# One decoder layer on one core: the gate r's last weight sum moved to a plain load and VectorE, its second step's blocks together, and the convolution's side work paced anew

## The chip, the cores and the metric

The kernel runs on 1 core of one Trainium2 chip. The metric is the device time of one execution in microseconds (us); lower is better. The kernel before took 844.33 us, the median of 3 runs (843.4 to 845.39). Engines are named as the profile names them: PE is TensorE, DVE is VectorE, ACT is ScalarE, POOL is GpSimd, SP is SyncE, which here only starts DMA transfers.

## The reference

One layer (DEPTH is 1) on 512 tokens of width 1024, all float32:

```
u = rmsnorm(x, norm1_g)
a_glu, q, k, v, r, g_low, gate_a, gate_b = split(u @ w_in)
c = a_glu[:, :1024] * sigmoid(a_glu[:, 1024:])
c = silu(layernorm(causal_dwconv(c, width 31)))          # convolution branch
o = gated linear attention, 4 heads, chunks of 64 (q, k, v, decay of g_low)
o = rmsnorm_per_head(o) * gla_norm_g * silu(r)            # r is the output gate
h = x + (sigmoid(gate_a) * (c @ w_conv_out) + sigmoid(gate_b) * (o @ w_gla_out)) @ w_o
h = h + ffn(rmsnorm(h, norm2_g));   out = rmsnorm(h, final_g)
```

The change lies in r = u @ w_r (1024 by 1024), in the depthwise convolution's taps beside the heads, and in the LayerNorm over channels that follows the convolution.

## The kernel before, in words

**Products in three terms.** Every float32 product is made of three fast ones: an operand x is split in a high half (ACT casts it to `whi`, L374 or L404) and a low half (DVE subtracts, `wlo`, L375 or L409); `mm3` (L463 to L469) issues low times high, high times low and high times high. So each weight block costs one ACT cast and one DVE subtraction before PE can use it. A flat list `order` (L213 to L243) says in which order weight blocks are loaded; `load` (L250) issues a block's DMA on SP's queue into one of 4 `raw` buffers, `refill` (L268) keeps up to 4 blocks (2 where marked tight) loaded ahead of the split ones, `split_weight` (L362) splits the next one into one of 4 `whi` and 4 `wlo` buffers, and `weight` (L427) hands a block to a product and splits up to LOOK = 2 ahead.

**Seven products in place of eight.** For r, w_o and w_down, `seven` (L1319) computes a 2 by 2 block product with seven block products (Winograd's form). Tokens are halved, the contraction is halved, the output columns are halved. The steps are a11, a12, s1, n2, s4, n3 and a22; each needs a sum of activation blocks (`token_sums_7`, L1137, on DVE and ACT) and a sum of weight blocks. Every step has two parts, d = 0 and 1, each with its own weight block (128 by 1024) that covers two pairs of contraction rows. A step with both parts at once makes 24 products of 512 columns; the list `STEPS` (L57) takes a11 whole, then a12 d0, s1 d0, a12 d1, s1 d1, and then n2, s4, n3, a22, each whole.

**The weight sums of r.** With W11, W12, W21, W22 the four blocks: a11 loads W11 into a `kept` buffer. After its split, POOL starts accumulating DMAs that add W12 to it (`sum_on`, L332, and `add_dram`, L297; for w_r each sum goes in two transfers of 256 KB). s1 uses that sum. a12 uses W21, loaded into `raw`. For n2, DVE adds the loaded W22 to `kept` (L329), giving W11 + W12 + W22; after n2's split POOL again starts accumulating DMAs, W21 on top, and a22 uses the result. s4 uses W22 alone, still in its `raw` buffer. n3 loads W12 into `raw`, and POOL's DMAs add W22. So POOL issues twelve transfers for r: four for s1, four for n3, four for a22.

**After each step** `put_r` (L1410) moves or combines the PSUM banks: ACT copies a11, s1, n2 (L1413); for a12, s4 and n3 DVE combines (L1420), ACT takes silu (L1421), DVE multiplies into the attention output `ot` (L1422); for a22 ACT takes silu from PSUM (L1416) and DVE multiplies. n2, n3 and a22 share one pair of banks, so a22's first product waits until n3's combination has read them. `weight` calls of a22 are placed after n3's second combination (`freed`, L1359). While r runs, sums of activations wait in `urgent`, and `fill` (L447) takes them ahead of convolution work.

**The convolution** is depthwise, width 31, on DVE: 44 taps per channel tile at half the tokens (L807; 0.6 share each; ACT starts each of the three sums, L803), three closing adds (L821 to L825), eight tiles. The taps are queued in `chains`, and every `weight` call hands out some with `fill`: `share` units, 5.0 (RATE) by default, 2.5 for the paired tiles, 2.0 for w_r. When the eighth tile is done, `add_chain` sums the eight tiles (L858, L861) on DVE, and `norm_chain` (L929) follows: `ln_parts` splits the sum (L920, L921), `ln_mean` multiplies it by -1/1024 on PE (L889), `ln_center` subtracts and squares per tile (L892 to L898), `ln_var` and `ln_rstd` make and spread the root (L868, L876), `ln_out` scales, takes silu and splits (L910 to L921). norm_chain is held (`hold`, L444) until `start_norms` (L1470), which runs in the third quarter of the first `pair_7`. Empty entries `(2.5, lambda: None)` in a chain are pauses.

**Order around the change.** Four heads (L1263 to L1281): queries and keys of head h, scores and outputs of head h - 1 on PE, the last three GLU tiles between. Then four `gate_b` tiles, r by `seven`, and from `pair_7(0)` on the gates of the merge in paired tiles: each pair loads two blocks ("x1": one, two), POOL adds up the other three (L346, `two_sums`), and PE takes them as x1, x3, x2, x4. In pair 0, `gated_o` transposes the attention output (L1115) and splits it to `oa` (L1122, L1123); then come w_gla tiles 0 and 1, and pair 1. `oa` number 3 lives in the buffer in which the taps' second operand `aside` stands, so it waits for the last tap. A scheduler decides the final order on each engine, except where `issue_after` and `keep_in_program_order` bind it; semaphores follow from it.

Of the kernel before, what the change touches and what calls it, by code (L numbers as in the profile page):

```python
# [37 lines left out]
R_PAIRS = ((0, 4), (1, 5), (2, 6), (3, 7))  # L38
# [9 lines left out]
RATE = 5.0  # L48
# [7 lines left out]

STEPS = [("a11", 0), ("a11", 1), ("a12", 0), ("s1", 0), ("a12", 1), ("s1", 1)]  # L57
STEPS += [(step, d) for step in ("n2", "s4", "n3", "a22") for d in (0, 1)]
START = {ET.PE, ET.Activation, ET.DVE, ET.SP}


# [16 lines left out]
def trunk_layer(ctx: ExitStack, tc: tile.TileContext, a: dict, out: bass.AP):  # L78
# [30 lines left out]
    def tmp(n=T):  # L109
        return tp.tile([P, n], F32, tag="tmp", name=nm("tmp"), bufs=6)  # L110
# [102 lines left out]
    order = [("w_v", j) for j in range(KT // 2)]  # L213
# [6 lines left out]
        if h:  # L220
            order += glu_order[KT - LATE_GLU + h - 1]
    order += [("w_gb", m) for m in range(AHEAD)]
    order += [("w_r", (R_PAIRS, step, d)) for step, d in STEPS]
    tight = set()
    first = len(order)
    for (name, p, q), behind in zip(MERGE, BEHIND):
# [48 lines left out]
    def raw_tile():  # L275
        return wp.tile([P, D], F32, tag="raw", name=nm("raw"), bufs=4)


    def block(name, pairs, d, row, col):

        pairs = pairs[2 * d : 2 * d + 2]
        first = pairs[0][row]
        if name == "w_r":
            tiles = a[name][4 * col : 4 * col + 4, :, first * P : (first + 2) * P]
            return tiles.rearrange("m p c -> p m c")
        w = a[name][col * SEVEN[name] + first // 2]
        return w if len(pairs) == 2 else w[:, row * T : (row + 1) * T]

    def keep_tile(name):
        if name in ("w_o", "w_r"):  # L290
            return tp.tile([P, D], F32, tag="x", name=nm("kept"), bufs=3)
        return fp.tile([P, D], F32, tag="kept", name=nm("kept"), bufs=2)
# [9 lines left out]
    LOADS = {"a11": (0, 0), "a12": (1, 0), "n2": (1, 1), "n3": (0, 1)}  # L302

    def load_block(name, pairs, step, d):

        if step not in LOADS:
            return None
        src = block(name, pairs, d, *LOADS[step])
        n = D if name == "w_r" else src.shape[-1]
        if step == "a11":  # L310
            dst = keep_tile(name)[:, :n]
            kept[pairs, d] = dst
        else:
            dst = raw_tile()[:, :n]
        load_dma = nc.sync.dma_start(shaped(name, dst), src)
        if name == "w_down":
            tc.keep_in_program_order(load_dma)
        if step == "n3":
            add_dram(name, dst, block(name, pairs, d, 1, 1))
        if step == "n2":  # L320
            kept[pairs, d, "b22"] = dst
        return dst

    def operand(raw, pairs, step, d):

        if step == "s4":
            return kept[pairs, d, "b22"]
        if step == "n2":
            nc.vector.tensor_tensor(kept[pairs, d], kept[pairs, d], raw, ALU.add)  # L329
        return raw if step in ("a12", "n3") else kept[pairs, d]  # L330

    def sum_on(name, pairs, step, d):  # L332

        if step in ("a11", "n2"):
            nxt = block(name, pairs, d, *((0, 1) if step == "a11" else (1, 0)))
            add_dram(name, kept[pairs, d], nxt)

# [89 lines left out]
    def weight(name, j, ahead=LOOK):  # L427
        assert order[used[0]] == (name, j)
        prefetch(1)
        used[0] += 1  # L430
        prefetch(ahead)
        share = {"two": 2.5, "w_glu": RATE + 0.75, "w_r": 2.0}.get(name, RATE)

        fill(share + (1.75 if order[min(len(ready), len(order)) - 1] in ADDED else 0))
        return ready[used[0] - 1]
# [4 lines left out]
    after, urgent, hold, conv_given = [], [], [True], []  # L440
# [6 lines left out]
    def fill(n):  # L447
        room[0] += n
        while (urgent or chains) and room[0] > 0:
            chain = urgent or chains[0]  # L450
            share, work = chain.pop(0)
            room[0] -= share
            with ExitStack() as order_of:
                for ins in (pace[0], *behind):
                    order_of.enter_context(tc.issue_after(ins.ins))
                work()
            if chains and not chains[0]:
                chains.pop(0)
                start_chain()
        if not chains and not urgent:  # L460
            room[0] = 0.0
# [108 lines left out]

    start = tc.manual_schedule(engines=START)
    start.__enter__()
# [355 lines left out]

    def norm_chain():  # L929
        chain = [(RATE, ln_parts)]  # L930
        chain.append((0, ln_mean))
        chain.extend((2, lambda k=k: ln_center(k)) for k in range(KT))
        chain += [(2.5, lambda: None)] * 4
        chain.append((RATE, ln_var))
        chain.append((2.5, lambda: None))
        chain.append((0, ln_rstd))
        chain.extend((2.5, lambda k=k: ln_out(k)) for k in range(KT))
        return chain
# [8 lines left out]
    raw = tmp()  # L947
# [313 lines left out]
    s1_n2, of_s1, s4, of_n2, of_s4, n3, of_n3 = merge_sums  # L1261
# [57 lines left out]
    def seven(name, pairs, acts, complete, at=lambda step, i: None, fine=False, put=None, before=lambda step: None):  # L1319
# [30 lines left out]
                    read = 2 * d + j == len(acts) - 1  # L1350
                    mm3(acc, (ah, al), w_, opens and d == 0 and j == 0, read, not opens)

        steps = list(STEPS)
        while steps:
            step, d = steps.pop(0)
            if d == 0:
# [7 lines left out]
            half, n, op, whole = into[step]  # L1364
# [71 lines left out]
    def pair_7(n):  # L1436
        (name, p, q), behind = MERGE[n], BEHIND[n]
        unit = two_tiles(name, p, q, lambda: merge_acts, mm_bank, len(behind) < 3)
        if behind and behind[0][0] == "w_conv":
            while chains:  # L1440
                fill(1)
        for j in range(4):
            while urgent and j and len(urgent) > (5 if j == 1 else 0):
                urgent.pop(0)[1]()
            done = next(unit)
            if n == 0 and j in (1, 2):
                for m in range(2 * j - 2, 2 * j):
                    gated_o(m, ax_bank)
                if j == 2:
                    start_norms()  # L1450
            if j == 0 or n >= 3:

                while complete_pairs:
                    complete_pairs.pop(0)()
            if j == 3:
                third_ahead()

                def sigmoids(done=done):
                    for m, c in zip((p, q), done):
                        (part if name == "w_gb" else gas)[m] = sigmoid(m, c)  # L1460

                complete_pairs.append(sigmoids)
                if n >= 3:
                    complete_pairs.pop()()
            for proj, m, half in behind[j : j + 1]:
                open_tiles[proj, m] = tile_of(proj, m, half_of[half], open_tiles.get((proj, m)))
# [37 lines left out]
    for p, q in O_PAIRS:  # L1504
# [6 lines left out]
        s1, n2, n3, s4 = e1[:, :H], e1[:, H:], e2[:, :H], e2[:, H:]  # L1511
# [201 lines left out]
    for gi, pairs in enumerate(GROUPS):  # L1713
        acts = []
        if gi == 0:
# [3 lines left out]
            for j, lo in [(j, lo) for lo in (0, H) for j in range(3)]:  # L1719
                late = {(1, 0): (KT - 1, 2), (2, 0): (MID, 3)}.get((j, lo))  # L1720
                at = {late[0]: lambda t=late[1]: to_channels(normed[t], u2, t)} if late else {}
# [6 lines left out]
            s1_n2, of_s1, s4, of_n2, of_s4, n3, of_n3 = sums  # L1728
# [135 lines left out]
```

## Time and profile before

| | |
|---|---|
| median of 3 runs | 844.33 us (843.4 to 845.39) |
| the profiled execution | 841.78 us, span 840.0 us |
| mean granted TensorE clock | 0.988 |
| PE busy | 809.8 us, 96% of the span |
| DVE busy | 713.6 us, 85% |
| ACT busy | 467.9 us, 56% |
| POOL busy | 171.1 us, 20% |
| HBM traffic | 137 GB/s over the span |

The profiled execution has 1.78 us around its span. The span's stages, by the windows of the trace: loading and v to about 43 us, GLU tiles with the taps, v and decay to about 113, the four heads to about 208, gate_b to 236, r from 236 to 292, pair 0 and the first two w_gla tiles to about 318, then the other gates, w_conv, w_o and the channel mixer. A row of the timeline gives start, duration, engine, line, operation, output and inputs, and in brackets how long the engine sat idle before it and what released it. A duration there includes the tail that overlaps the next instruction; start to start is a little shorter.

### The profile page before, as it was taken

The numbers are of one execution on the slowest core, as the hardware profiler recorded it, in microseconds if no ns is written. First come the engines' busy times: TensorE is split into PE (matmuls) and PEld (weight loads), VectorE is DVE, ScalarE is ACT, GpSimd is POOL, SyncE is SP. The second block draws the span as 40 slices with busy tenths as digits, with TensorE's granted clock in tenths as the row PEclk, the third lists the DMA queues.
The fourth block names the chain that finished last, engine by engine and source line by source line (L and its number), as shares of the span: only waits on it lengthen the run. The fifth ranks groups of instructions, "written<-read, shape, count | busy, mean of one in ns | idle before, by whom it ended". The sixth has DMA issues, their size and how long they took to land.

```text
span 840.0 us, 11519 instructions
## 1 busy us (share of the span) xinstructions
PE 809.8 (96%) x4263; PEld 698.1 (83%) x4263; DVE 713.6 (85%) x1162; ACT 467.9 (56%) x690; POOL 171.1 (20%) x157
## 2 busy tenths in 40 slices
PE   9999999999998498999999999999999999999996
PEld 7888887888886387999988898899889988899885
DVE  6789999999877597576768889988974999779895
ACT  6654684764554454495444556546534664456654
POOL 2011011212122323323200110221212311422012
PEclk9999999999999699999999999999999999999999
DMA  8488868648455222325248732135663266424662
GB/s 331 136 199 190 217 155 195 145 108 200 76 101 125 42 96 89 101 76 176 92 139 214 207 101 80 47 101 181 130 165 101 89 168 144 139 98 153 177 126 100
DMA packets 38680, 115.70 MB, mean 138 GB/s; under 512 B 3848, under 2 KB 11152, under 8 KB 38624
## 3 DMA queue, kind: packets, MB, share of 16 engines
q1 hardware_dynamic: 27856, 85.34, 29.5%
q0 software_dynamic: 10752, 29.63, 21.0%
q8 instruction: 33, 0.54, 0.3%
q14 instruction: 23, 0.19, 0.1%
q10 hardware_dynamic: 16, 0.00, 0.0%
HBM read 112.86 MB, written 2.10 MB: 137 GB/s over the span
## 4 chain that ended last, share of the span: by engine, by line
PE 74%; DVE 17%; issue 3%; ACT 2%; POOL 2%; DMA 1%; POOLq 0%; SPq 0%; DVEq 0%; ACTq 0%
PE mm L467 21%; PE mm L468 21%; PE mm L469 21%; DVE c L807 6%; DVE aside L807 3%; PE mm L681 3%; PE ax L469 2%; PE ax L467 2%; PE ax L468 2%; DVE wlo L375 2%; POOL raw L346 1%; DMA raw<-in_w_v_dram 1%; DMA kept<-in_w_r_dram 1%; DVE h L842 0%; PE ax L1077 0%
## 5 line engine op out<-in xcount | busy, mean ns | idle before, releaser
L467 PE MATMUL mm<-uh,wlo 128*128 128x512 f32 (+1 forms) x608 | 220.1, 362 | 0.0
L468 PE MATMUL mm<-ul,whi 128*128 128x512 f32 (+1 forms) x608 | 218.1, 359 | 0.0
L469 PE MATMUL mm<-uh,whi 128*128 128x512 f32 (+1 forms) x608 | 217.8, 358 | 0.0
L469 PEld LDWEIGHTS mm<-uh,whi 128*128 128x128 f32 x608 | 115.4, 190 | 17.0
L467 PEld LDWEIGHTS mm<-uh,wlo 128*128 128x128 f32 x608 | 115.6, 190 | 16.6
L468 PEld LDWEIGHTS mm<-ul,whi 128*128 128x128 f32 x608 | 115.5, 190 | 16.3
L375 DVE TENSOR_TENSOR wlo<-raw,whi 128x1024 fp32r<-128x1024 f32 x86 | 100.2, 1171 | 33.6 <-ACT whi L374 29.8
L346 POOL TENSOR_TENSOR raw<-raw,raw 128x512 f32<-128x512 f32 x42 | 66.9, 1592 | 235.4 <-DVE wlo L375 152.7
L374 ACT CAST whi<-raw 128x1024 fp32r<-128x1024 f32 x86 | 82.4, 964 | 37.0 <-PE mm L469 26.6
L404 ACT CAST whi<-raw 128x1024 fp32r<-128x1024 f32 x78 | 81.4, 1046 | 32.2 <-PE mm L469 13.3
L409 DVE TENSOR_TENSOR wlo<-raw,whi 128x1024 fp32r<-128x1024 f32 x50 | 66.6, 1335 | 7.5 <-ACT whi L404 7.3
L374 ACT CAST whi<-kept 128x1024 fp32r<-128x1024 f32 (+1 forms) x40 | 40.2, 1008 | 51.3 <-DMA kept<-in_w_r_dram 17.0
L375 DVE TENSOR_TENSOR wlo<-kept,whi 128x1024 fp32r<-128x1024 f32 (+1 forms) x40 | 46.5, 1165 | 16.5 <-ACT whi L374 16.4
L807 DVE SCALAR_TENSOR_TENSOR c<-h,pp,c 128x255 f32<-128x255 f32 (+14 forms) x120 | 57.5, 479 | 2.6 <-ACT c L803 2.5
L807 DVE SCALAR_TENSOR_TENSOR c<-aside,btmp,c 128x255 f32<-128x255 f32 (+14 forms) x120 | 58.5, 488 | 0.0
L406 ACT ACTIVATE wlo<-raw 128x1024 fp32r<-128x1024 f32 x28 | 29.6, 1060 | 49.1 <-PE mm L467 40.4
L807 DVE SCALAR_TENSOR_TENSOR aside<-h,pp,aside 128x255 f32<-128x255 f32 (+6 forms) x112 | 53.7, 479 | 0.0
L1588 DVE SCALAR_TENSOR_TENSOR tmp<-mm,pp,tmp 128x511 f32<-128x511 f32 (+1 forms) x56 | 41.4, 742 | 4.0 <-ACT tmp L1585 3.9
L1209 ACT COPY tmp<-mm 128x256 f32<-128x256 f32 x48 | 17.6, 368 | 41.7 <-PE mm L469 41.2
L1370 DVE TENSOR_TENSOR hres<-hres,mm 128x512 f32<-128x512 f32 (+1 forms) x49 | 32.3, 670 | 3.8 <-PE mm L469 3.5
L467 PE MATMUL mm<-whi,ul 128*128 128x512 f32 x48 | 19.5, 406 | 14.4 <-DVE r L1420 14.4
L1585 ACT ACTIVATE tmp<-mm,pp 128x512 f32<-128x512 f32 x28 | 21.8, 777 | 19.1 <-PE mm L469 18.9
(384 smaller groups left out, 1908.8 us busy)
## 6 DMA issues: line engine op xcount, KB each, us to landing
raw<-in_w_up_dram SPq DMA_DIRECT2D x44, 512.0 KB, 3.7
raw<-in_w_glu_dram SPq DMA_DIRECT2D x16, 512.0 KB, 5.5
raw<-in_w_down_dram SPq DMA_DIRECT2D x15, 512.0 KB, 4.7
wlo<-in_w_glu_dram POOLq DMA_DIRECT2D x12, 512.0 KB, 7.0
kept<-in_w_down_dram POOLq DMA_DIRECT2D x10, 512.0 KB, 5.5
raw<-in_w_v_dram SPq DMA_DIRECT2D x8, 512.0 KB, 6.9
raw<-in_w_qk_dram SPq DMA_DIRECT2D x8, 512.0 KB, 6.4
wlo<-in_w_qk_dram POOLq DMA_DIRECT2D x8, 512.0 KB, 7.3
```

The lines of the kernel that those rows point to most:

```text
L346: work = nc.gpsimd.tensor_tensor(out, x, y, ALU.add)
L374: nc.scalar.copy(hi, raw)
L375: two_low[:] = [nc.vector.tensor_tensor(lo, raw, hi.bitcast(F32), ALU.subtract)]
L404: nc.scalar.copy(hi, raw)
L406: pace[0] = nc.scalar.mul(lo, raw, -1.0)
L409: pace[0] = nc.vector.tensor_tensor(lo, raw, hi.bitcast(F32), ALU.subtract)
L467: nc.tensor.matmul(acc, ll, rh, start=first, stop=False, **kw)
L468: nc.tensor.matmul(acc, lh, rl, start=False, stop=False, **kw)
L469: nc.tensor.matmul(acc, lh, rh, start=False, stop=last, **kw)
L807: nc.vector.scalar_tensor_tensor(out[:, j:], x[:, : half_t - j], w, out[:, j:], ALU.mult, ALU.add)
L1370: done = nc.vector.tensor_tensor(hres[t, n][:, c], hres[t, n][:, c], acc[:, c], op)
L1588: nc.vector.scalar_tensor_tensor(z[:, s:], acc[:, : T - s], w[j], z[:, s:], ALU.mult, ALU.add)
```

## The change

1. w_r gets its own list of steps with every step whole: a12 d0, a12 d1, then s1 d0, s1 d1.
2. The last weight sum of r: W21 for a22 is loaded by SP into two more `raw` buffers, and DVE adds it to `kept` ahead of a22's split, in place of POOL's four accumulating DMAs after n2's split.
3. `weight` hands out other shares beside the heads: 1.0 for the first head's two blocks (5.0 before), 6.0 for the other six (5.0 before). Where the block split ahead is an "added" one, 1.75 comes on top as before.
4. Two more pauses of 2.5 between `ln_parts` and `ln_mean`.
5. In pair 0, at its third quarter, taps that are left are issued until only norm_chain is left in `after`.

```
+R_STEPS = [(step, d) for step in ("a11", "a12", "s1", "n2", "s4", "n3", "a22") for d in (0, 1)]
-    order += [("w_r", (R_PAIRS, step, d)) for step, d in STEPS]
+    order += [("w_r", (R_PAIRS, step, d)) for step, d in R_STEPS]
     def load_block(name, pairs, step, d):
-        if step not in LOADS:
+        at = LOADS.get(step, (1, 0) if (name, step) == ("w_r", "a22") else None)
+        if at is None:
             return None
-        src = block(name, pairs, d, *LOADS[step])
+        src = block(name, pairs, d, *at)
     def operand(raw, pairs, step, d):
-        if step == "n2":
+        if step == "n2" or step == "a22" and raw is not None:
             nc.vector.tensor_tensor(kept[pairs, d], kept[pairs, d], raw, ALU.add)
     def sum_on(name, pairs, step, d):
-        if step in ("a11", "n2"):
+        if step == "a11" or step == "n2" and name != "w_r":
     def weight(name, j, ahead=LOOK):
         share = {"two": 2.5, "w_glu": RATE + 0.75, "w_r": 2.0}.get(name, RATE)
+        if name == "w_qk":
+            share = 1.0 if j < 2 else RATE + 1.0
     def norm_chain():
         chain = [(RATE, ln_parts)]
+        chain += [(2.5, lambda: None)] * 2
         chain.append((0, ln_mean))
     def seven(...):
-        steps = list(STEPS)
+        steps = list(R_STEPS if name == "w_r" else STEPS)
     def pair_7(n):
             done = next(unit)
+            if n == 0 and j == 2:
+                while len(after) > 1:
+                    fill(1)
```

In the built program the counts are these: SP issues 2 DMAs more (the two loads of 512 KB), POOL 4 fewer, DVE has 2 additions of 128 by 1024 more, PE and ACT keep their instructions. What stands where on each engine also moves: in the changed program 11 taps fewer stand on DVE ahead of the first head's keys, and the next head's scan (L1021) and one subtraction (L1028) stand ahead of them in return; 4 taps that stood ahead of a12's first split stand behind a22's last one, where there are now 18 (14 before); in the r stage DVE has the h products of a12 (L1422) ahead of n2's first split; and PE's mean product stands behind all 24 products of pair 1's x1 (before, within them).

## The prediction

> **What bounds the kernel now.** First the page: PE is busy 96% of the span, so what PE waits for is all that a change of order can win.
>
> ```profile
> PE 809.8 (96%) x4263; PEld 698.1 (83%) x4263; DVE 713.6 (85%) x1162; ACT 467.9 (56%) x690; POOL 171.1 (20%) x157
> PEclk9999999999999699999999999999999999999999
> ```
>
> One slice of 40 shows a low granted clock: the fourteenth, 273 to 294 us. Second, PE's timeline from 130 to 330 us: its waits (in brackets: idle before, releaser), a11's first product at 236.06, and n3's last two, whose starts lie 0.22 to 0.23 us apart:
>
> ```profile
> 131.92 0.55 PE L1057 MATMUL ax<-ident,k 128*128 128x128 f32 x3 [1.84 <-DVE k L1051]
> 236.06 0.39 PE L467 MATMUL mm<-whi,ul 128*128 128x512 f32 x1
> 254.78 0.73 PE L467 MATMUL mm<-whi,hq 128*128 128x512 f32 x2 [0.88 <-ACT whi L374]
> 269.93 0.39 PE L468 MATMUL mm<-wlo,sumsq 128*128 128x512 f32 x1
> 270.15 0.39 PE L469 MATMUL mm<-whi,sumsq 128*128 128x512 f32 x1
> 284.99 0.76 PE L467 MATMUL mm<-whi,ul 128*128 128x512 f32 x1 [14.45 <-DVE r L1420]
> 305.23 0.47 PE L467 MATMUL mm<-oa,wlo 128*128 128x512 f32 x1 [0.97 <-ACT oa L1122]
> 321.72 0.50 PE L889 MATMUL ax<-sum,shares 128*128 128x512 f32 x1 [3.17 <-ACT sum L920]
> 325.96 0.40 PE L467 MATMUL mm<-oa,wlo 128*128 128x512 f32 x1
> ```
>
> The large wait stands ahead of a22, the last step of r. The releaser named is n3's combination (L1420), but DVE's, ACT's and POOL's rows show why that came so late:
>
> ```profile
> 264.33 1.21 POOL L300 DMA_DIRECT2D kept<-in_w_r_dram  x1 [3.92 <-issue]
> 271.12 1.20 POOL L300 DMA_DIRECT2D kept<-in_w_r_dram  x1 [5.58 <-issue]
> 275.72 1.21 POOL L300 DMA_DIRECT2D kept<-in_w_r_dram  x1 [3.40 <-issue]
> 270.90 1.04 ACT L374 CAST whi<-kept 128x1024 fp32r<-128x1024 f32 x1 [8.78 <-DMA kept<-in_w_r_dram]
> 280.21 1.04 ACT L374 CAST whi<-kept 128x1024 fp32r<-128x1024 f32 x1 [8.27 <-DMA kept<-in_w_r_dram]
> 240.14 1.23 DVE L375 TENSOR_TENSOR wlo<-kept,whi 128x1024 fp32r<-128x1024 f32 x1 [5.71 <-ACT whi L374]
> 262.47 2.36 DVE L375 TENSOR_TENSOR wlo<-raw,whi 128x1024 fp32r<-128x1024 f32 x2
> 271.97 1.22 DVE L375 TENSOR_TENSOR wlo<-kept,whi 128x1024 fp32r<-128x1024 f32 x1 [5.95 <-ACT whi L374]
> 281.82 1.29 DVE L1422 TENSOR_TENSOR h<-h,r 128x512 f32<-128x512 f32 x2 [8.62 <-ACT r L1421]
> 284.16 1.28 DVE L1420 TENSOR_TENSOR r<-r,mm 128x512 f32<-128x512 f32 x2
> ```
>
> POOL issues its four accumulating transfers for a22 one after another, some 4.6 us apart from 271.12 to 275.72; ACT's casts wait for their landings at 270.90 and 280.21, and silu, DVE's products and n3's combination stand behind them in line.
>
> Third, the windows: before, inside and behind.
>
> ```profile
> 240.00:266.00 26.00, 25.06 (x109) 19.92 (x108) 25.86 (x33) 16.65 (x24) 6.77 (x6) 1.00 0.54 113
> 266.00:284.00 18.00, 4.54 (x21) 3.42 (x19) 3.43 (x5) 4.08 (x5) 6.18 (x5) 0.73 0.42 71
> 130.00:134.00 4.00, 2.16 (x16) 1.00 1.08 268
> 285.00:288.00 3.00, 3.00 (x7) 0.50 0.03 5
> 322.00:326.00 4.00, 4.00 (x21) 0.57 0.53 177
> ```
>
> In the first two rows the third busy figure is DVE's: 25.86 of 26 us up to 266, then 3.43 of 18. So r is bound by DVE up to 266 us, and by POOL's transfers after that. The last three rows are of PE alone; their clock (third figure from the right) is 1.00 behind the wait of 1.84 us, 0.50 behind 14.45 and 0.57 behind 3.17.
>
> **The change part by part.** PE's whole loss from 130 to 326 us is 1.84 + 0.88 + 14.45 + 0.97 + 3.17 = 21.3 us of waits, and 3.0 x 0.50 + 4.0 x 0.43 = 3.2 us of slow clock: 24.5 us. That would be the gain if PE never waited. DVE does not allow it, so the sum goes by DVE.
>
> *The weight sum by load and VectorE.* POOL's four transfers go. SP issues two loads more, into `raw` buffers that are free once s4's blocks are split: by the second row of L375 above, whose two instructions are n3's splits, s4's stand just ahead, so the loads can start from about 259 and 261 us. How long they take is bounded by two groups:
>
> ```profile
> raw<-in_w_gb_dram SPq DMA_DIRECT2D x8, 512.0 KB, 3.4
> raw<-in_w_r_dram SPq DMA_DIRECT2D x6, 512.0 KB, 7.9
> ```
>
> So they land at 263 to 267 and 265 to 269 us. The medians of w_r include queueing behind others; I take the lower. DVE's queue reaches the additions at 267: from its restart it first has 11 instructions of 128x1024 (9 splits, n2's 2 additions) and 23 of 128x512, 240.5 + 11 x 1.15 + 23 x 0.61 = 267.2. So the loads are hidden; with 7.9 us each DVE would wait up to 2 us per block, 4 in all. Behind them on SP's queue stand pair 0's two loads, whose buffers come free with n3's splits; they land by about 270, and are wanted only after a22. Each addition is one 128x1024 DVE instruction: L375's pair above takes 2.36 us, so about 1.15 each, 2.3 us in all; 0.61 is the like for 128x512 (284.16: 1.28 for two, with overlap).
>
> *Whole steps.* The work stays; its order moves. a12's second block is split first, when DVE restarts at 240.14; s1's both follow, and n2's first split comes behind a12's combinations and products. Down DVE's new queue n2's first block is ready at 240.5 + 5 x 1.15 + 13 x 0.61 = 254.2 and its second, 2 long and 3 short ones on, at 258.3. PE wants the first at 251.1: it comes to r 1.84 us earlier, a11, a12 and s1 are 72 products of 0.228 (236.06 - 1.84 + 16.4 = 250.6), and a12's second block is some 0.5 late. So PE waits about 3 and, 12 products later, 1.3 us in n2, where it waited 0.88. This is inside DVE's ledger and not charged twice.
>
> *Fewer taps beside the first head.* The keys come 2.4 us earlier on DVE (11 taps less, a scan and a subtraction more), so the 1.84 us at 131.92 go. PE then reaches r 1.84 us earlier and waits there for DVE: alone worth nothing, bounds 0 and 1.84. The 4 taps that move behind a22 cost DVE's later stretch 4 x 0.48 (488 ns by the row below) = 1.9 us.
>
> ```profile
> L807 DVE SCALAR_TENSOR_TENSOR c<-aside,btmp,c 128x255 f32<-128x255 f32 (+14 forms) x120 | 58.5, 488 | 0.0
> ```
>
> *The mean later, the flush of taps.* In the built order both change little on DVE: the taps are spread between the same splits. PE's two mean products come behind all of pair 1's x1, so of the 4.24 us from 321.72 to 325.96, in which PE does both and the rest of x1 at a slow clock, only one mean product (0.50) is left behind the wait.
>
> **DVE's ledger.** From its restart at 240.14 to the end of the sum's low half (321.70 + 0.69 = 322.39, rows below) DVE spends 82.25 us.
>
> ```profile
> 290.56 1.50 DVE L807 SCALAR_TENSOR_TENSOR c<-aside,btmp,c 128x244 f32<-128x244 f32 x1
> 293.41 0.75 DVE L1123 SCALAR_TENSOR_TENSOR h<-ax,pp,h 128x512 fp32r<-128x512 f32 x1 [0.36 <-ACT h L1122]
> 294.51 2.07 DVE L1123 SCALAR_TENSOR_TENSOR h<-ax,pp,h 128x512 fp32r<-128x512 f32 x3 [0.35 <-ACT h L1122]
> 317.52 1.23 DVE L375 TENSOR_TENSOR wlo<-raw,whi 128x1024 fp32r<-128x1024 f32 x1 [2.27 <-ACT whi L374]
> 321.70 0.69 DVE L921 TENSOR_TENSOR sum<-btmp,sum 128x512 fp32r<-128x512 f32 x1
> ```
>
> Idle in it: 5.95 + 8.62 + 0.36 + 0.35 + 2.27 = 17.55, so work is 64.7. Added: 2.3 (additions), 1.9 (taps), 0.6 (one activation sum that now stands behind the restart). The restart itself hangs on ACT's casts behind the four gated copies that wait for POOL; I keep it, with 0.4 us for a different order of casts. The sum is then ready at 240.5 + 69.5 = 310.0. PE: one more mean product, 0.5, and w_gla tile 2 starts at 310.5, where it started at 325.96. Gain **15.5 us**. What is late next: n2's splits (4.3 us of PE), a22's start behind n3's combinations and its own split (about 1.4), w_gla tiles 0 and 1 behind DVE's splits and the last taps (about 3): some 9 of the 24.5 us come back as smaller waits, which is the same sum seen from PE.
>
> [...]
>
> [...] Pair 0's sums, on POOL beside an idle DVE before, now run beside a busy one. The rows:
>
> ```profile
> 276.48 3.08 POOL L346 TENSOR_TENSOR raw<-raw,raw 128x512 f32<-128x512 f32 x2
> 309.69 6.71 POOL L346 TENSOR_TENSOR raw<-raw,raw 128x512 f32<-128x512 f32 x2 [17.90 <-DVE wlo L409]
> ```
>
> Two sums took 3.08 us beside the idle DVE and 6.71 beside the busy one. From 270 on they end at 277, not 273, and with a cast and a split at about 280; PE wants x3 at about 282 (a22 from 272 to 278, 16 transposes, then x1's 24 products of 256 columns, half of 0.228 each). I cost it at nothing; without that slack it is 3.6 us.
>
> **The bounds.** The profiled execution took 841.78, so the sum gives 826.3; the median of the runs is 2.55 above that execution, and results are compared with runs: 844.33 - 15.5 = **828.8**. Above: if DVE restarts 1.84 us earlier with PE, and stretches inside its work close (the tap at 290.56 took 1.50 where 0.48 is usual: 1.0), the gain is 18.3; beyond that lies rival 1. Below: loads of 7.9 us (4) and a slow clock in n2 (1.7): 9.8.
>
> **Rivals.**
>
> 1. *DVE is not the bound, PE runs nearly dry.* Gain 18 to 24: 820.3 to 826.3. For it: waits hidden in DVE's rows. Against: 25.86 of 26 us.
> 2. *The wait goes elsewhere.* The loads land late, POOL's sums or n2's splits hold PE: gain 3 to 13, 831.3 to 841. For it: 7.9 us, and the 3.6 us above.
> 3. *The change doesn't do what it says.* If the loads, four buffers back in SP's queue, only start after n3 is done, a22 waits as before: the 14.45 us stay, gain about 1, 843. Against: s4's splits free the buffers by 262.
> 4. *Slower, by the LayerNorm.* The mean moves 5 shares down a chain that ends in the last low half of the convolution, and that one has little room:
>
> ```profile
> 382.91 1.78 DVE L921 TENSOR_TENSOR c<-btmp,ch 128x512 fp32r<-128x512 f32 x1
> 390.84 0.40 PE L467 MATMUL mm<-ch,wlo 128*128 128x512 f32 x1
> ```
>
> Before, the last of eight was done at 384.7 and the first was wanted at 390.84: 6 us. Two `weight` calls later is about 5.6 us (48 products of 256 columns). If the shift were larger, PE would wait at w_conv one for one; it decides from 6 + 15.5 = 22 us of slip, and at 25 the time is 847.
>
> **How the numbers follow.** Forecast (gain 13 to 18, 826.3 to 831.3): 0.58. Rival 1: 0.12; rival 2: 0.23; rival 3: 0.03; rival 4: 0.04. The range 824 to 835 holds the forecast and the inner parts of rivals 1 and 2. A measurement of this kernel can tell about 0.2% (1.7 us) from no change; within it lies rival 3. So faster 0.93, same 0.03, slower 0.04.
>
> **What would show it.** Right: no POOL transfer for r after n3's; a22 starts within 2 us of n3's end; DVE over 95% busy from 240 to 305 us; PE's waits in n2 some 4 us; no wait at L889 over 1 us; clock 1.00 throughout. Wrong: a wait of over 5 us ahead of a22 (the loads), DVE idle in the r stage (rival 2), or a wait at the first w_conv product (rival 4).

## The result, and the profile after

The changed kernel takes **834.68 us** (median of 4 runs, 834.35 to 836.2) against 844.82 for the kernel before in the same measurement: ratio 0.9886, 95% interval 0.9868 to 0.9904. That is 10.1 us faster. The forecast was 828.8, with a range of 824 to 835: the direction held, the time lies 5.9 us above the forecast and at the upper end of the range. The profiled execution took 834.76 (span 833.0), within 0.1 us of the median; the profiled execution of before took 841.78, so the two traces lie 7.0 us apart.

Line numbers of the changed kernel are 1 to 8 higher (L375 is L377, L807 is L811, L889 is L893, L1115 is L1120, L1420 to L1422 are L1425 to L1427); each kernel below has its own. From the page:

```profile
PE 813.0 (98%) x4263; PEld 697.5 (84%) x4263; DVE 723.1 (87%) x1164; ACT 466.9 (56%) x690; POOL 169.3 (20%) x153
PEclk9999999999999999999999999999999999999999
```

The slice with the low clock is gone. PE's timeline from r to the mean's second product, with all its waits over 0.8 us, and the first product of w_gla tile 2 last:

```profile
236.00 0.39 PE L471 MATMUL mm<-whi,ul 128*128 128x512 f32 x1
254.90 0.50 PE L471 MATMUL mm<-whi,hq 128*128 128x512 f32 x1 [0.95 <-ACT whi L376]
256.72 0.50 PE L472 MATMUL mm<-wlo,hq 128*128 128x512 f32 x1 [1.32 <-DVE wlo L377]
273.64 0.39 PE L473 MATMUL mm<-whi,sumsq 128*128 128x512 f32 x1
274.93 0.47 PE L471 MATMUL mm<-whi,ul 128*128 128x512 f32 x1 [0.24 <-DVE r L1425]
286.30 0.38 PE L471 MATMUL mm<-hq,wlo 128*128 128x256 f32 x1 [1.97 <-ACT tmp L1214]
296.91 0.66 PE L1120 MATMUL ax<-ident,h 128*128 128x128 f32 x4 [0.88 <-DVE oa L1128]
298.79 0.47 PE L471 MATMUL mm<-oa,wlo 128*128 128x512 f32 x1 [1.23 <-DVE wlo L411]
316.81 0.51 PE L893 MATMUL ax<-sum,shares 128*128 128x512 f32 x1 [1.20 <-ACT sum L924]
318.49 0.50 PE L893 MATMUL ax<-sum,shares 128*128 128x512 f32 x1 [1.18 <-DVE sum L925]
318.83 0.39 PE L471 MATMUL mm<-oa,wlo 128*128 128x512 f32 x1
```

The 14.45 us ahead of a22 are 0.24, and a22 starts 10.06 us earlier. Between a22 and w_gla tile 2, 2.9 of these are given back: from 274.93 to 318.83 are 43.9 us, and before the change (284.99 to 325.96) it was 40.97. The windows show that DVE is now the full engine (behind the window and its length stand the busy times of PE, PE's weight loads, DVE, ACT and POOL, each with its number of instructions):

```profile
243.00:266.00 23.00, 19.51 (x80) 14.77 (x81) 22.93 (x30) 16.68 (x24) 4.18 (x4) 1.00 0.49 100
266.00:284.00 18.00, 17.76 (x95) 14.97 (x94) 18.00 (x22) 9.12 (x12) 6.39 (x4) 1.00 0.33 108
284.00:305.00 21.00, 15.66 (x98) 13.51 (x98) 19.85 (x36) 10.97 (x17) 2.85 (x2) 0.92 0.29 101
```

What DVE and POOL do there, in rows of the changed kernel's timeline. DVE first: its restart in r (the first instruction behind its long wait there), the two new additions, and rows that are longer than their shapes take elsewhere (two products of 128x512 1.29 us, a tap 0.47, a split 1.22, an addition 0.68):

```profile
243.07 1.23 DVE L377 TENSOR_TENSOR wlo<-raw,whi 128x1024 fp32r<-128x1024 f32 x1 [9.11 <-ACT whi L376]
269.40 1.23 DVE L331 TENSOR_TENSOR kept<-kept,raw 128x1024 f32<-128x1024 f32 x1
272.96 1.22 DVE L331 TENSOR_TENSOR kept<-kept,raw 128x1024 f32<-128x1024 f32 x1
276.51 3.49 DVE L1427 TENSOR_TENSOR h<-h,r 128x512 f32<-128x512 f32 x2
284.12 1.47 DVE L811 SCALAR_TENSOR_TENSOR c<-aside,btmp,c 128x245 f32<-128x245 f32 x1
306.01 2.31 DVE L411 TENSOR_TENSOR wlo<-raw,whi 128x1024 fp32r<-128x1024 f32 x1
308.24 3.23 DVE L865 TENSOR_TENSOR btmp<-btmp,c 128x512 f32<-128x512 f32 x3
313.72 2.38 DVE L865 TENSOR_TENSOR btmp<-btmp,c 128x512 f32<-128x512 f32 x2
```

And POOL: the last transfer that stands ahead of the fourth head's root (`rstd`, 128x4, the inverse root for that head's norm), that root, and gate_b's sums for pairs 0 and 1:

```profile
237.75 1.20 POOL L301 DMA_DIRECT2D kept<-in_w_r_dram  x1 [4.69 <-issue]
238.50 1.51 POOL L523 TENSOR_TENSOR rstd<-mean,mhalf 128x4 f32<-128x4 f32 x1
273.09 4.66 POOL L348 TENSOR_TENSOR raw<-raw,raw 128x512 f32<-128x512 f32 x2 [15.08 <-DVE wlo L377]
277.71 1.74 POOL L348 TENSOR_TENSOR raw<-raw 128x512 f32<-128x512 f32 x1
283.90 1.43 POOL L348 TENSOR_TENSOR raw<-raw,raw 128x512 f32<-128x512 f32 x1 [4.45 <-DVE wlo L377]
303.47 3.77 POOL L348 TENSOR_TENSOR raw<-raw,raw 128x512 f32<-128x512 f32 x2 [18.14 <-ACT whi L406]
307.20 2.27 POOL L348 TENSOR_TENSOR raw<-raw 128x512 f32<-128x512 f32 x1
313.88 1.68 POOL L348 TENSOR_TENSOR raw<-raw,raw 128x512 f32<-128x512 f32 x1 [4.42 <-DVE wlo L377]
```

Each long DVE row lies across the end of one of POOL's sums. PE's wait of 1.97 us at 286.30 comes from these sums as well, by way of ACT: the copy that PE waited for stands behind a cast that waited 3.49 us for POOL's sum of 283.90.

```profile
285.36 0.62 ACT L376 CAST whi<-raw 128x512 fp32r<-128x512 f32 x1 [3.49 <-POOL raw L348]
285.88 0.37 ACT L1214 COPY tmp<-mm 128x256 f32<-128x256 f32 x1
```

DVE's ledger, made again as in the prediction (every DVE instruction from the restart to the end of the sum's low half, its usual start-to-start length by shape, idle time, and what is left over as stretch):

| kernel | restart | work | stretch | idle | sum ready |
|---|---|---|---|---|---|
| before | 240.14 | 60.95 | 3.76 | 17.55 | 322.39 |
| prediction | 240.5 | 65.75 | 3.76 | 0 | 310.0 |
| changed | 243.07 | 66.51 | 7.71 | 1.15 | 318.44 |

So the sum was late by 2.57 (restart) + 0.76 (work) + 3.95 (stretch) + 1.15 (idle) = 8.4 us. Work and stretch rest on what is taken as a usual length; another choice moves up to 0.9 us between these two, but not their sum. The theory to be tested was that two of these are causes of their own: the heavier shares of taps beside heads 2 to 4 push the restart back, and POOL's sums make DVE stand still. The rivals: something else stretches these rows; another engine sets the end; or the parts of the change that carry the gain are not the weight sum.

### The profile page after: what moved, and what is told of

The parts are those of the page before. It is cut to its first block, busy times and chain, and to the rows that moved or that the text cites. A ratio compares the mean times of both kernels' runs of the same rounds, so it can differ in the third digit from the quotient of the medians.

```text
span 833.0 us, 11507 instructions
## 1 busy us (share of the span) xinstructions
PE 813.0 (98%) x4263; PEld 697.5 (84%) x4263; DVE 723.1 (87%) x1164; ACT 466.9 (56%) x690; POOL 169.3 (20%) x153
## 4 chain that ended last, share of the span: by engine, by line
PE 83%; DVE 10%; issue 4%; ACT 2%; POOL 1%; POOLq 0%; DVEq 0%; ACTq 0%
PE mm L471 23%; PE mm L472 23%; PE mm L473 23%; PE mm L685 3%; PE ax L473 2%; PE ax L472 2%; PE ax L471 2%; DVE wlo L377 2%; DVE c L811 1%; DVE h L1427 1%; DVE tmpq L1170 1%; DVE aside L811 1%; DVE kept L331 1%; DVE wlo L411 1%; DVE btmp L865 1%
## 5 line engine op out<-in xcount | busy, mean ns | idle before, releaser
L377 DVE TENSOR_TENSOR wlo<-raw,whi 128x1024 fp32r<-128x1024 f32 x86 | 101.6, 1187 | 33.1 <-ACT whi L376 31.1
L348 POOL TENSOR_TENSOR raw<-raw,raw 128x512 f32<-128x512 f32 x42 | 64.0, 1524 | 248.1 <-DVE wlo L377 145.3
L411 DVE TENSOR_TENSOR wlo<-raw,whi 128x1024 fp32r<-128x1024 f32 x50 | 68.3, 1369 | 7.7 <-ACT whi L406 7.7
L811 DVE SCALAR_TENSOR_TENSOR c<-h,pp,c 128x255 f32<-128x255 f32 (+14 forms) x120 | 57.3, 478 | 1.6 <-ACT c L807 1.5
L811 DVE SCALAR_TENSOR_TENSOR c<-aside,btmp,c 128x255 f32<-128x255 f32 (+14 forms) x120 | 58.4, 486 | 0.0
L811 DVE SCALAR_TENSOR_TENSOR aside<-h,pp,aside 128x255 f32<-128x255 f32 (+6 forms) x112 | 53.5, 478 | 0.0
L377 DVE TENSOR_TENSOR wlo<-kept,whi 128x1024 fp32r<-128x1024 f32 (+1 forms) x40 | 46.7, 1167 | 5.5 <-ACT whi L376 5.4
L348 POOL TENSOR_TENSOR raw<-raw 128x512 f32<-128x512 f32 x14 | 30.2, 2160 | 0.0
```

What stands on the lines that cost most here:

```text
L348: work = nc.gpsimd.tensor_tensor(out, x, y, ALU.add)
L377: two_low[:] = [nc.vector.tensor_tensor(lo, raw, hi.bitcast(F32), ALU.subtract)]
L411: pace[0] = nc.vector.tensor_tensor(lo, raw, hi.bitcast(F32), ALU.subtract)
L811: nc.vector.scalar_tensor_tensor(out[:, j:], x[:, : half_t - j], w, out[:, j:], ALU.mult, ALU.add)
```

## The experiments

Each kernel was timed against the kernel before in five rounds; medians of before there were 842.07 to 843.86.

### The old shares

```
         share = {"two": 2.5, "w_glu": RATE + 0.75, "w_r": 2.0}.get(name, RATE)
-        if name == "w_qk":
-            share = 1.0 if j < 2 else RATE + 1.0
```

> The changed kernel (834.68 us) with the old shares of taps beside the heads (5.0 for every w_qk block). In the changed kernel DVE restarts in r at 243.07 us, where 240.14 was the time before. Theory A (the restart slipped because the heavier shares of heads 2 to 4 push the last head's mean back, and with it POOL's root and ACT's casts): the restart returns to 240 to 241, 4 taps fewer stand behind it, the sum of the eight tiles is ready 2.5 to 4.5 us earlier, PE waits 1.8 us again at about 132 us, and the time is 830 to 832.5. Rival B (the shares help: keys earlier, PE at r earlier): the time is 835 to 837.

Measured: 830.01 us (829.46 to 830.43), ratio 0.9836 (0.9823 to 0.985), which lies clear of the changed kernel's 0.9868 to 0.9904. So, by the medians, the new shares cost 4.7 us of the gain. PE's timeline, with the wait that the shares were to save, and the end of the sum:

```profile
132.04 0.55 PE L1060 MATMUL ax<-ident,k 128*128 128x128 f32 x3 [1.71 <-DVE k L1054]
236.19 0.39 PE L469 MATMUL mm<-whi,ul 128*128 128x512 f32 x1
314.07 0.39 PE L469 MATMUL mm<-oa,wlo 128*128 128x512 f32 x1
```

The wait is back, yet a11 starts at 236.19 where it started at 236.00: what PE saved at 132 us it had lost again before r. Of 4.76 us by which the sum is ready earlier (313.68), 1.1 are the restart (241.97), 3.3 are work (four taps, one split and one sum of activations that no longer stand in this stretch), 2.0 are stretch (5.69), and idle time takes back 1.66. The amount is theory A's, the restart's part of it smaller than A said.

### POOL's sums for gate_b left out

```
         raws = pair_raws[name, p]
+        if name == "w_gb" and part == "x3":
+            return raws[0]
...
+        if name == "w_gb":
+            if part == "x1":
+                pair_raws[name, p].append(pair_raws[name, p][1])
+            return
```

> The changed kernel with POOL's eight sums for pairs 0 and 1 of gate_b left out: the second, third and fourth products of these pairs take loaded blocks as they are, so the gate_b tiles 4 to 7 are not those of the reference; DVE, ACT and PE keep their instructions. In the changed kernel ten DVE instructions beside these sums are stretched (two products of 128x512 take 3.49 us, a tap 1.47, a split 2.31), some 7 us in all. Theory A (POOL's sums slow DVE, and DVE sets the end of the sum): the stretched rows return to 1.3, 0.5 and 1.2 us, the sum is ready 5 to 7 us earlier, the time is 828 to 831. Rival B (the stretch comes from something else, or PE's waits are ACT's): the rows stay, the time is within 1.5 us of 834.7.

Measured: 829.26 us (827.72 to 829.45), ratio 0.9824 (0.981 to 0.9837). DVE's timeline, the same products, split and additions as in the changed kernel's rows above:

```profile
276.84 1.29 DVE L1433 TENSOR_TENSOR h<-h,r 128x512 f32<-128x512 f32 x2
301.49 1.22 DVE L417 TENSOR_TENSOR wlo<-raw,whi 128x1024 fp32r<-128x1024 f32 x1
302.62 2.14 DVE L871 TENSOR_TENSOR btmp<-btmp,c 128x512 f32<-128x512 f32 x3
```

3.49 has become 1.29, 2.31 has become 1.22, 3.23 has become 2.14. The ledger: work 66.51 as in the changed kernel, stretch 1.31 for 7.71, sum ready at 311.62. The restart stays where it was (242.88), so this is the sums alone; PE's wait at 286 us is gone with them. Theory A is shown: POOL's eight sums cost DVE 6.4 us, and 5.4 of these reach the end.

### The weight sum alone

The kernel before with the second part of the change only (the `load_block`, `operand` and `sum_on` lines of the diff).

> The kernel before (844.8 us) with the weight sum alone changed: the last sum of r by a plain load and a DVE addition, all else as before. Theory A (the weight sum carries the gain, the other parts are worth little by themselves): the 14.45 us wait goes but for 2 to 4 us, DVE restarts at about 240 as before, the mean's wait of about 3 us at a slow clock stays; gain 7 to 10, time 835 to 838. Rival B (the new order of steps, the shares or the later mean carry a good part): gain under 6, time above 839. Rival C (the other parts cost more than they bring): time under 834.

Measured: 832.2 us (829.06 to 834.46), ratio 0.9855 (0.9834 to 0.9877): rival C. By the medians the weight sum alone gains 11.3 us, more than all five parts together; the two intervals overlap a little, so "at least as much" is what is shown. Its runs spread over 5.4 us, and its profiled execution, the highest of them, shows where; POOL's timeline, the roots of the first two heads:

```profile
152.72 4.65 POOL L520 TENSOR_TENSOR rstd<-mean,mhalf 128x4 f32<-128x4 f32 x1 [4.67 <-DVE mean L1102]
182.96 3.02 POOL L520 TENSOR_TENSOR rstd<-mean,mhalf 128x4 f32<-128x4 f32 x1 [7.53 <-DVE mean L1102]
```

In the kernel before both took 1.19 in its profiled execution. Here DVE's restart came at 244.54; of all the traces only the two with the mean on POOL, below, have a later one.

### The last root ahead of two transfers

```
-                    for ins in behind:
+                    for ins in behind + (roots_at if (name, spec[1:]) == ("w_r", ("a11", 1)) else []):
                         order_of.enter_context(tc.issue_after(ins.ins))
                     sum_on(name, *spec) if name in SEVEN else two_sums(*spec)
```

> The changed kernel with one thing moved: on POOL the root of the last head (rstd) stands ahead of the two accumulating transfers of a11's second block, not behind them; all other engines have the same instructions in the same order. In the changed kernel the mean is ready at 232.0 us, the root comes at 238.50 behind POOL's transfers, ACT's four copies at 240.05, its cast at 241.97, and DVE restarts at 243.07 after 9.11 us idle. Theory A (DVE's restart sets the end of the sum): the root comes at 232 to 234, DVE restarts at 236 to 238, then waits 1 to 3 us for the s1 sum of the second block, whose transfers start 1.5 us later; the sum is ready 3 to 6 us earlier and the time is 829 to 832. Rival B (another engine sets the end): DVE restarts earlier and waits elsewhere, time within 1 us of 834.7.

Measured: 836.21 us (835.31 to 836.61), ratio 0.991 (0.9897 to 0.9924), so no gain and rather a loss: theory A falls as it stood, and the sum is ready at 318.62, no earlier than in the changed kernel. Three engines' rows of its timeline, POOL's root and the last transfer for n3, ACT's cast for n3, and DVE's restart with its two waits:

```profile
232.01 2.59 POOL L523 TENSOR_TENSOR rstd<-mean,mhalf 128x4 f32<-128x4 f32 x1 [3.59 <-DVE mean L1106]
258.97 1.21 POOL L301 DMA_DIRECT2D raw<-in_w_r_dram  x1 [3.39 <-issue]
265.46 1.05 ACT L376 CAST whi<-raw 128x1024 fp32r<-128x1024 f32 x1 [2.98 <-DMA raw<-in_w_r_dram]
237.66 1.23 DVE L377 TENSOR_TENSOR wlo<-raw,whi 128x1024 fp32r<-128x1024 f32 x1 [3.94 <-ACT whi L376]
246.16 1.23 DVE L377 TENSOR_TENSOR wlo<-kept,whi 128x1024 fp32r<-128x1024 f32 x1 [3.13 <-ACT whi L376]
267.06 1.30 DVE L1183 TENSOR_TENSOR hq<-tmpq,sumsq 128x512 fp32r<-128x512 f32 x2 [3.30 <-ACT sumsq L1178]
```

DVE restarts 5.4 us earlier and waits 3.1 for s1's second sum and 3.3 behind ACT, whose cast waits for n3's last transfer, issued 2.2 us later than in the changed kernel (258.97 for 256.80). So an early restart was worth nothing here, where POOL's chain of eight transfers, most of them 4.5 to 5 us apart, came later in return: root and transfers stand in the same queue.

### The shares and the flush alone

The kernel before with the third and fifth part of the change only (shares and flush).

> The kernel before (843.5 to 844.8 us) with the new shares of taps beside the heads and the flush of taps alone. In the changed kernel these shares cost 4.7 us. Theory A (they cost because DVE sets the end there; in the kernel before POOL's transfers set a22's start, and DVE idles 14.6 us in that stall, so that the four taps behind it cost little, and the 1.84 us wait ahead of the keys goes): 843 to 846. Rival B (the shares lose time in the head phase itself, whatever comes later): 847 to 850.

Measured: 846.87 us (845.87 to 847.65), ratio 1.0038 (1.0024 to 1.0051): slower by 3.3 us, between A's range and B's. PE's and POOL's timelines have a22's start and the last transfer that it waits for:

```profile
288.83 0.77 PE L469 MATMUL mm<-whi,ul 128*128 128x512 f32 x1 [13.61 <-DVE r L1422]
279.68 1.21 POOL L300 DMA_DIRECT2D kept<-in_w_r_dram  x1 [3.50 <-issue]
```

The wait at 132 us is gone here too, the restart comes at 243.11, and the last transfer at 279.68, not 275.72; a22 follows, 3.8 us later than before. So the shares cost through POOL's chain where that sets the end, and through DVE's restart and work where DVE does. Both start from one slip: the fourth of POOL's transfers, ahead of the last root, starts at 237.79 here and at 237.75 in the changed kernel, where it was 234.82 before. This run has the flush of taps as well, which was not tried by itself.

### Without the two pauses; with the old order of steps

Both on top of the kernel with the old shares; the first takes the line `chain += [(2.5, lambda: None)] * 2` out, the second puts `STEPS` back in both places of `R_STEPS`.

> The changed kernel with the old shares (830.01 us) and without the two pauses ahead of the LayerNorm mean. Theory A (the later mean is worth what PE loses beside it, as the prediction says): PE's two mean products come back into pair 1's x1, and a wait of 2 to 3 us at L889's place comes with a slow clock behind it; 831.5 to 834. Rival B (PE waits for DVE anyway, whichever product it waits with): within 1 us of 830.

Measured: 832.05 us (831.18 to 832.24), ratio 0.9861 (0.9845 to 0.9876), 2.0 us more than with them, though the two intervals overlap a little. The mean's first product in PE's timeline:

```profile
313.61 0.50 PE L891 MATMUL ax<-sum,shares 128*128 128x512 f32 x1 [3.19 <-ACT sum L922]
```

Theory A's size, and half of its reason: the wait of 3.2 us is back, but from 311 to 326 us the clock stays at 1.00. w_gla tile 2 starts 2.0 us behind the end of the sum (316.31 and 314.28), where it was 0.4 with the pauses (314.07 and 313.68).

> The changed kernel with the old shares (830.01 us) and with the old order of steps in r (a12 d0, s1 d0, a12 d1, s1 d1). Theory A (the order of steps does not change DVE's work, which sets the end): within 1.5 us of 830. Rival B (whole steps spare PE or ACT waits): 832 to 834. Rival C (whole steps cost something, as n2's splits come late): 826 to 828.5.

Measured: 830.52 us (829.62 to 831.13), ratio 0.9845 (0.9829 to 0.9861): theory A. The order of steps makes no difference that can be told.

### POOL's sums on DVE

```
-            work = nc.gpsimd.tensor_tensor(out, x, y, ALU.add)
+            work = (nc.vector if name == "w_gb" else nc.gpsimd).tensor_tensor(out, x, y, ALU.add)
```

Once on the changed kernel, once on that with the old shares.

> The changed kernel (834.68 us), its shares as they are, with POOL's eight sums for pairs 0 and 1 of gate_b as DVE instructions. There the rows beside these sums are 6.4 us longer than usual (7.7 less the 1.3 left in the run without the sums). Theory A: 8 x 0.6 = 4.8 us of DVE more, 6.4 less: gain 1 to 2.5, 832 to 833.7. Rival B (no gain, since what DVE takes on is what it gets back): 834 to 836.

> The changed kernel with the old shares (830.01 us) and, beside that, POOL's eight sums for pairs 0 and 1 of gate_b as DVE instructions. In the run with the old shares DVE's rows between its restart in r and the end of the eight-tile sum are 5.7 us longer than usual, 1.3 in the run without POOL's sums. Theory A (the price of POOL's sums is that DVE stands still beside them): DVE takes 8 x 0.6 = 4.8 us more and loses 4.4 us of stretch, so the sum is ready at about the same time; 829 to 831.5, and no DVE row beyond its usual length. Rival B (the sums cost DVE less than the rows say): 832 to 835. Rival C (ACT's and PE's waits for POOL's sums were the larger part): under 828.5.

Measured: 832.0 us (831.21 to 832.35), ratio 0.9857 (0.984 to 0.9875), and 828.64 us (826.37 to 830.7), ratio 0.9826 (0.9807 to 0.9844): theory A for the first, and between A's range and C's for the second. Stretch is 1.0 and 0.8 us. DVE takes eight additions more, and the time falls by 2.7 and 1.4. The second is the version with the lowest median, 6.0 us below the changed kernel; its interval overlaps that of the old shares alone. Its profiled execution, the lowest of its runs, has the first three roots at 1.19 to 1.20 us and the restart at 240.19.

### The heads' small addition on POOL

```
-            nc.vector.tensor_scalar(v, ss, EPS, None, ALU.add)
+            nc.gpsimd.tensor_scalar(v, ss, EPS, None, ALU.add)
```

On the changed kernel, and on that with the old shares and the sums on DVE.

> The changed kernel (834.68 us) with the heads' small addition ahead of the root (mean, 128x4) on POOL instead of DVE. With the new shares the mean of the second head reached POOL's root at 183.43 us, with the old ones at 180.4 to 180.7, and DVE's restart in r came at 242.9 to 243.1 against 240.1 to 242.5. Theory A (the slip goes through DVE's queue: more taps stand ahead of the mean): the roots start 1 to 3 us earlier, the restart comes at 240 to 241.5, the time is 831.5 to 833.5. Rival B (POOL's small instructions are held by DVE's taps: the root took 1.2, 1.9, 3.0 or 4.7 us in one and the same place of these runs): two of them are held longer, the roots end later, 835 to 838.

> The kernel with the old shares and gate_b's sums on DVE (828.64 us, 826.37 to 830.7) with the heads' small addition on POOL as well. Theory A (mean and root no longer wait for DVE's queue): restart at 239 to 240, 826 to 828 and a narrower spread. Rival B (POOL's small instructions are held by DVE's taps): the restart and the times spread as before or more, 829 to 832.

Measured: 835.42 us (834.65 to 838.66), ratio 0.9926 (0.9908 to 0.9943), and 832.87 us (832.04 to 833.08), ratio 0.9887 (0.9869 to 0.9904): rival B. The first lies by its time among the changed kernel's runs (834.35 to 836.2) and by its ratio just above that kernel's interval, so at best nothing was won; the second is clearly slower, 4.2 us above the kernel that it was made from. POOL's timeline of the first, the third head's addition beside DVE's taps and the fourth's beside an idle DVE:

```profile
207.07 6.41 POOL L1106 TENSOR_SCALAR mean<-ss 128x4 f32<-128x4 f32 x1 [3.43 <-ACT junk L1104]
242.25 0.22 POOL L1106 TENSOR_SCALAR mean<-ss 128x4 f32<-128x4 f32 x1
```

And DVE's timeline of the same kernel, the first and the last of 17 taps in a row, start to start 0.38 to 0.39, and the instruction after them:

```profile
206.80 0.47 DVE L811 SCALAR_TENSOR_TENSOR c<-h,pp,c 128x246 f32<-128x246 f32 x1
212.94 0.46 DVE L811 SCALAR_TENSOR_TENSOR c<-aside,btmp,c 128x241 f32<-128x241 f32 x1
213.43 0.43 DVE L825 TENSOR_TENSOR c<-c,aside 128x256 f32<-128x256 f32 x1
```

An addition of four columns, 0.22 us beside an idle DVE, took 6.41 and came through as DVE's taps ended (207.07 + 6.41 = 213.48). The other additions of the first three heads in these two kernels took 4.36, 5.04, 6.00 and 6.33 us, each until a row of taps, or the one instruction behind it, was over, and once only 1.25 (184.27 to 185.52), where a DVE instruction of 128x4 at 185.33 broke the row.

### A gap for the root

On the kernel with the old shares and the sums on DVE, for the first three heads, a copy on DVE that waits for POOL's root:

```
+            if self.h < HEADS - 1:
+                with tc.manual_schedule(engines={ET.DVE, ET.Pool}):
+                    nc.vector.tensor_scalar(v, ss, EPS, None, ALU.add)
+                    root = rsqrt(v, NT)
+                    r = small(NT, "rstd")
+                    nc.vector.tensor_copy(r, root)
...
```

> The kernel with the old shares and gate_b's sums on DVE (828.64 us, single runs from 826.37 to 830.7), and for the first three heads a 128x4 copy of POOL's root on DVE, one tap behind the mean, so that DVE stands idle until the root is done. Theory A (POOL's small instruction gets through when DVE pauses; where DVE's taps run without a break it waits 1.2 to 4.7 us by chance): each root takes 1.0 to 1.5 us in every execution, DVE loses 0.5 to 1 us per head, the restart in r comes at 240 to 241, the time is 826.5 to 828.5 and the single runs lie within 1.5 us. Rival B (the pauses cost what they bring): 828.5 to 830. Rival C (the lengths of the root have another cause): the roots still vary and the runs spread over 3 us or more.

Measured: 829.63 us (829.39 to 829.98), ratio 0.9832 (0.9815 to 0.9849). The signs are theory A's: the three roots took 1.20, 1.19 and 1.12 us, and the runs lie within 0.6 us where they spread over 4.3. They do not prove it: one execution was profiled, and the runs of the kernel with the old shares alone, which has no such gap and a root of 3.02 us, lie within 1.0 us. The time is rival B's: DVE stands idle 0.93 to 0.94 us each time, a11 starts 1.3 us later than in that kernel's execution (237.73 for 236.46), and the restart is at 243.77.

## Why the prediction failed, point by point

- **What bounds, and that the wait goes:** right. No POOL transfer for r follows n3's; a22 starts 1.3 us behind n3's last product (forecast within 2); DVE is 99.7% busy from 243 to 266, 100% to 284 and 94.5% to 305. The weight sum alone brings all of the gain (11.3 us).
- **The loads are hidden:** right. They start at 261.9, and neither addition waits for a transfer; the additions take 1.13 us start to start.
- **Whole steps:** right in kind. PE's waits in n2 are 0.95 + 1.32 + 0.37 (forecast 3 and 1.3), with clock 1.00 behind them; the order is worth nothing by itself. With the mean on POOL the same two waits, 0.95 and 1.32, had 0.50 behind them (the rows are below). The 1.7 us that the range keeps for a slow clock in n2 is a figure that no run shows: behind these waits nothing was lost in the changed kernel (clock 1.00), and about 1.5 us with the mean on POOL, where seven products took 3.1 us (260.29 to 263.38) and 0.228 each makes 1.6.
- **The step that failed first, "I keep it, with 0.4 us":** DVE's restart. It came at 243.07, 2.57 us late. Its chain runs through the heads: DVE's mean, POOL's root, ACT's copies and casts, the split of a11, POOL's four transfers, the last root. The prediction weighed the shares only at their two ends, the 1.84 us wait and four taps, and let the six heavier blocks between pass. Of the 2.93 us by which the restart is later than before (243.07 for 240.14), 1.75 are there when the first of the four transfers starts (222.53 for 220.78); the rest arises at the fourth, which starts 5.87 us behind the third, for 4.6 before, and the profile names nothing that it waited for, so this part stays open. With the new shares the restart lies at 242.9 to 243.2 in all four profiled executions in which mean and root were left as they are (the changed kernel, POOL's sums left out, POOL's sums on DVE, the shares alone). With the old shares it was 240.1 and 240.2 where the first roots took 1.2 us, and 242.0 to 244.5 where one or two of them took 3.0 or 4.65 (the kernel with the gap for the root left aside). The figure 240.14 was that of an execution with short roots.
- **The step that failed most, "I cost it at nothing":** POOL's sums. The prediction asked only how long POOL's sums would take beside a busy DVE (6.71 us for 3.08), and when PE would want x3. The runs show the other side: DVE's own rows are lengthened, 6.4 us over eight sums, 3.95 more than in the kernel before, where three of pair 0's sums ran while DVE was idle in the stall. A row of before already showed it: the tap of 1.50 us at 290.56, beside POOL's sum of 290.40, which the prediction named and put down as a possible gain.
- **The mean later:** right in kind. The forecast was 4.24 - 0.50 = 3.7 us, 1.7 of them from the slow clock; the experiment gave 2.0, without a slow clock there. Both of PE's products still wait, 1.20 and 1.18, as the sum came 8 us later than forecast.
- **No new slow clock:** wrong once. Behind the waits of 1.97 and 0.50 us at 286 and 287 the clock was 0.68 (286 to 288) and then 0.50 (288 to 290), some 1.6 us. The first of them is from POOL's last sum for pair 0, by way of ACT.
- **LayerNorm's slack, and the flush:** the first held. The last low half is done at 382.7 and w_conv starts at 383.74 without a wait; of the 6 us that were there 1 is left. The flush of taps was not tried by itself.
- **The span against the median:** the prediction took before's profiled execution 2.55 below its median and kept that distance. The changed kernel's execution is within 0.1 us of its median, so 2.55 of the 8.4 us do not show in the medians: 8.4 - 2.55 = 5.9. That before's execution lay low because its roots were short is argued from the roots of the others, not shown.

The time came from rival 2's direction (a wait goes elsewhere), but by none of the prices that it named: not late loads, not n2, and POOL's sums cost through DVE's rows, not by keeping PE from x3.

## What to carry to other kernels

When a stall goes, look at what ran beside the idle engine while it lasted: here GpSimd's sums, three of which ran beside an idle VectorE before, lengthened VectorE's rows by 6.4 us once VectorE was busy, and in the changed kernel the same sums were cheaper on VectorE itself (832.0 us for 834.68). A change that evens out one engine's work far ahead of the bottleneck has to be followed through every queue to the stage that pays, and leaving it out may be the better version: here the plain weight sum carried the whole gain. A start time read from one execution is a sample: in the six kernels with the old shares and no gap for the root, DVE's restart lay anywhere from 240.1 to 244.5 us.

## What the runs showed of the hardware that was not expected

**GpSimd's small instructions took up to 6.4 us beside VectorE's taps.** With the old shares the first head's root (128x4) took 1.2 us in most executions and 4.65 in two, and the second's 1.2 or 3.0. The 128x4 addition took 0.22 beside an idle DVE, and 4.36 to 6.41 in five of six cases beside taps. A tap takes 0.39 us start to start; the addition of 6.41 ran beside 16 of 17 taps in a row and ended at 213.48, where the instruction behind the last tap starts at 213.43. In the other direction DVE's rows were 1.0 to 1.1 us longer for each of POOL's sums that ended in them: two products of 128x512 took 3.49 for 1.29 across two such ends, a tap 1.47 for 0.47, a split 2.31 for 1.22.

**In these runs a longer wait did not always have the lower clock behind it.** In the kernel without the two pauses a wait of 2.71 us ended at 285.77 and one of 3.19 at 313.61. PE's windows behind the first and behind the second (the clock is the third figure from the right):

```profile
287.00:289.00 2.00, 2.00 (x11) 0.50 0.00 0
314.00:318.00 4.00, 4.00 (x28) 1.00 0.53 184
```

The longer wait cost no clock, the shorter one half of it; the 3.17 us of before had 0.57 behind it. Waits of the same length differ too: n2's two waits of 0.95 and 1.32 us had 1.00 behind them in the changed kernel (first row, from 257 us) and 0.50 in that kernel with the mean on POOL (second row, from 261 us):

```profile
257.00:259.00 2.00, 1.63 (x8) 1.00 0.15 14
261.00:263.00 2.00, 2.00 (x6) 0.50 0.43 48
```

Products of 512 columns start 0.43 us apart behind these two waits in the changed kernel with the mean on POOL (260.88 to 262.59), where 0.23 is usual; in the changed kernel with POOL's sums on DVE, behind waits of 0.91 and 1.32, they do so as well (257.38 to 259.94). What decides between the two clocks no run shows.
